# Operands of the seven-product MLP taken from one transposition of each row tile, and its start in a written order

## Chip, cores and metric

The kernel runs on one core of one Trainium2 chip. The metric is the device time of one execution in microseconds (us), the median of several runs of the same program. TensorE (PE) multiplies matrices and transposes 128x128 blocks, VectorE (DVE), ScalarE (ACT) and GpSimd (POOL) work on tiles, and the queue of SyncE (SP) issues the loads and stores.

## What is computed

The reference is an encoder of two layers on 1024 tokens of 1024 channels. Layer 0 begins with an attention over the tokens, layer 1 with a pooling mixer. Each layer then attends into 256 memory tokens (`memory_cross_attention`) and applies a gated MLP. The change lies in these last two steps:

```
def memory_cross_attention(h, mem_n, w_q, w_kv, w_o):
    q = (h @ w_q).reshape(b, s, X_HEADS, X_HEAD_DIM) * (X_HEAD_DIM ** -0.5)
    ...
    p = jax.nn.softmax(scores, axis=-1).astype(v.dtype)
    o = jnp.einsum('bhsm,bmhd->bshd', p, v).reshape(b, s, D_MODEL)
    return o @ w_o

def conv_gated_ffn(h, w_up, conv_w, conv_b, w_down):
    u = h @ w_up
    up = jnp.pad(u, ((0, 0), (1, 1), (0, 0)))
    u = up[:, :-2] * conv_w[0] + up[:, 1:-1] * conv_w[1] + up[:, 2:] * conv_w[2] + conv_b
    gate, val = u[..., :D_FF], u[..., D_FF:]
    return (jax.nn.silu(gate) * val) @ w_down

# per layer
    x = x + memory_cross_attention(rmsnorm(x, xattn_norm[i]), rmsnorm(mem, mem_norm[i]), ...)
    x = x + conv_gated_ffn(rmsnorm(x, ffn_norm[i]), ...)
```

All of it is float32. D_FF is 2816, so that `w_up` is 1024 x 5632: 22 blocks of 128 gate columns and 22 of value columns.

## The kernel before

**Arithmetic.** Each operand of a matrix product is kept as two float32 parts of fewer bits, `hi` and `lo`. `hi_lo` (L150) makes them: ACT copies the source to `hi` (L153), VectorE subtracts it from the source (L154). A product of 128x128 with 128x512 is then three matmuls in `mm3` (L230; hi·hi L233, hi·lo L234, lo·hi L235). The split operands lie in 20 slots of a pool `R`, raw data in six tiles `scr` and in the eight tiles `X` of the residual (128 tokens x 1024 channels each). PSUM has a pool `psA` of two tiles of two banks and `psB` of four banks.

**Cross-attention and output projection.** `cross` (L624 on) makes scores, softmax and values; what it returns is the transposed output, one group of slots for the first 512 tokens, one for the second. `project` (L248) multiplies it with `w_o`: for each column half n of `w_o` (loaded and split just before its use), for each of the 8 row tiles, 24 matmuls into one bank, and VectorE adds the bank to `X` (L261). In the second half each row tile is then stored to DRAM (`Xd`, L723), since the residual is needed again behind the MLP and its tile in SBUF is used up, and normed in place (square sum on ACT, GpSimd, VectorE L219). One tile later its blocks are transposed.

**The MLP by seven products.** `seven_into` (L706), `ffn` (L750) and `ffn_main` (L831) compute the up-projection with Strassen's scheme in Winograd's form. The weights of pair f (128 gate and 128 value columns) give A11, A12 (gate, first and second half of the channels), A21, A22 (value); the normed rows give B11, B21 (first 512 tokens, by channel half), B12, B22 (second 512 tokens). The sums are S1 = A21 + A22, S2 = S1 - A11, S4 = A12 - S2, S3 = A11 - A21, and T1 = B12 - B11, T2 = B22 - T1, T3 = B22 - B12, T4 = B21 - T2. Seven products of 12 matmuls each replace eight:

- p2 = A12·B21 goes to a bank of its own and is copied into the gate row (ACT)
- p1 = A11·B11 opens the bank z and is added to the gate row (VectorE, L817)
- p5 = S1·T1 opens the bank y and is copied into the value row (ACT, L879)
- p6 = S2·T2 accumulates in z; z is copied into the gate row (ACT, L882)
- p3 = S4·B22 accumulates in y; y is added to the gate row (VectorE, L885)
- p7 = S3·T3 accumulates in z; z is added to the value row (VectorE, L890)
- p4 = A22·T4 accumulates in z; z is copied into the value row (ACT, L896)

The two rows of 128 x 1024 then pass through the convolution (ACT L841, VectorE L842 and L843), SiLU (ACT L887) and the product of gate and value (VectorE L902), and are stored to DRAM as a row of `G` (L903). The order of the products of pair f is p1, p5, p6, p3, p7, p2 of pair f+1, p4. Between them stand the splits of the seven left operands of pair f+1 (`ahead`), and at the end of a pair the load of the weights of pair f+2 (L771, two tiles of 512 KB) and their four sums on GpSimd (L782 to L785).

**The operands on the right.** T1, T2, T3, T4 are made from the rows before they are transposed, on VectorE and GpSimd (`second`, L725 on). Seven operands of four tiles with four blocks each are transposed (L718), 112 blocks per layer; T3 and T4 come after the products p2 and p1 of pair 0 (`tail`). T2 has a tile of its own, `extra`.

**Behind it.** The down-projection (`down`, `operand` L849) takes G back from DRAM in rounds of four rows.

**What sets the order.** Most of the program is given to a scheduler, which sets the order of the instructions on each engine by its own costs; within an engine the queue is then fixed, and each instruction waits for what it reads and for buffers. Only parts under `manual_schedule` keep the order of the source.

## Time and profile before

| | |
|---|---|
| median of 3 runs | 2659.68 us (2658.92 to 2660.28) |
| the profiled execution | 2661.13 us, its span 2659.4 us |
| mean granted TensorE clock | 0.992 of full speed |
| TensorE matmuls and transposes | 2595.0 us, 98% of the span, 13913 instructions |
| TensorE weight loads | 2216.8 us, 83%, 13913 instructions |
| VectorE | 1720.5 us, 65%, 2291 instructions |
| ScalarE | 1207.8 us, 45%, 2024 instructions |
| GpSimd | 695.0 us, 26%, 709 instructions |
| DMA | 209.22 MB, mean 79 GB/s |

The span is the time between the first and the last event of the profiled execution; the time of the execution is a little longer. Busy shares are means over the whole span. The output projection and the start of the MLP lie near 845 to 1000 us in layer 0 and near 1870 to 2020 us in layer 1. A row of busy time by stretches has the bounds and the length of the stretch, then for PE, weight loads, VectorE, ScalarE and GpSimd the busy time with the number of instructions begun, then the granted clock (1.00 is full), the DMA share and the GB/s. A row of waits names the waiting instruction, behind the arrow what it waited for, and then the time in us, the number of waits and the longest. A row of instructions in a timeline has start, duration, engine, line, operation and tiles, the number of instructions that the row joins (their duration is then from the first start to the last end), and in brackets the idle time before it.

### The profile page before, as it was taken

Reading aid. Unit: us, or ns where it says so; the run is one execution under the profiler, and the core shown is the slowest. Engines: PE = TensorE matmul, PEld = TensorE weight load, DVE = VectorE, ACT = ScalarE, POOL = GpSimd, SP = SyncE. Lnnn points to the kernel's source line nnn. Section 1 sums busy time; section 2 is a strip of 40 time slices with the busy share of each in tenths; the row PEclk is TensorE's granted clock in tenths of the full one; section 3 lists DMA queues with packets and bytes.
Section 4 is the critical chain, followed back from the end, with each engine's and each line's share of the span. In section 5 each row is a group of like instructions: output and inputs, shape, how many; then the busy total and the mean of one; then the engine's idle time right before and its main releaser. Section 6 shows DMA issues by size and latency. Waiting matters only on the chain.

```text
span 2659.4 us, 36296 instructions
## 1 busy us (share of the span) xinstructions
PE 2595.0 (98%) x13913; PEld 2216.8 (83%) x13913; DVE 1720.5 (65%) x2291; ACT 1207.8 (45%) x2024; POOL 695.0 (26%) x709
## 2 busy tenths in 40 slices
PE   8989999999999999999999998999999999999998
PEld 7988888888898878888878888889878888887886
DVE  6779999955246387777765435425378777767434
ACT  4448888843135255454542205425245555444111
POOL 3664445521012153433300001102034333310001
PEclk9999999999999999999999999999999999999999
DMA  4200000032222132223254203322122232326201
GB/s 157 83 1 1 1 1 1 2 135 65 70 80 89 48 95 73 94 72 95 87 187 154 100 19 89 103 64 72 58 92 91 72 95 72 95 104 241 99 24 63
DMA packets 167554, 209.22 MB, mean 79 GB/s; under 512 B 6741, under 2 KB 134077, under 8 KB 167381
## 3 DMA queue, kind: packets, MB, share of 16 engines
q1 hardware_dynamic: 167381, 206.91, 23.4%
q8 instruction: 109, 1.79, 0.3%
q14 instruction: 64, 0.52, 0.1%
HBM read 166.42 MB, written 35.65 MB: 76 GB/s over the span
## 4 chain that ended last, share of the span: by engine, by line
PE 57%; DVE 2%; ACT 2%; DMA 1%; issue 1%; POOL 1%; SPq 0%; POOLq 0%; DVEq 0%; ACTq 0%
PE pB L234 18%; PE pB L233 18%; PE pB L235 18%; DVE R L154 1%; ACT R L153 1%; DMA scr<-X 0%; DMA scr<-G 0%; PE pA L998 0%; PE pA L233 0%; PE pA L234 0%; PE pA L235 0%; DVE scr L842 0%; PE pB L718 0%; POOL ms L206 0%; DVE scr L843 0%
## 5 line engine op out<-in xcount | busy, mean ns | idle before, releaser
L233 PE MATMUL pB<-R,R 128*128 128x512 f32 (+1 forms) x3088 | 1160.9, 377 | 16.5 <-ACT scr L879 9.6
L234 PE MATMUL pB<-R,R 128*128 128x512 f32 (+1 forms) x3088 | 1157.6, 375 | 4.3 <-DVE R L154 4.0
L235 PE MATMUL pB<-R,R 128*128 128x512 f32 (+1 forms) x3008 | 1125.6, 374 | 0.0
L233 PEld LDWEIGHTS pB<-R,R 128*128 128x128 f32 x3088 | 582.1, 189 | 127.6 <-ACT scr L879 10.4
L234 PEld LDWEIGHTS pB<-R,R 128*128 128x128 f32 x3088 | 582.7, 189 | 109.0 <-DVE R L154 7.5
L235 PEld LDWEIGHTS pB<-R,R 128*128 128x128 f32 x3008 | 567.5, 189 | 101.0 <-DVE R L154 0.4
L153 ACT ACTIVATE R<-scr 128x1024 fp32r<-128x1024 f32 (+1 forms) x186 | 185.7, 1024 | 353.0 <-PE pB L234 283.5
L154 DVE TENSOR_TENSOR R<-X,R 128x512 fp32r<-128x512 f32 x294 | 256.3, 885 | 63.6 <-ACT R L153 63.0
L153 ACT ACTIVATE R<-X 128x512 fp32r<-128x512 f32 x294 | 181.3, 630 | 245.4 <-PE pB L234 225.6
L922 DVE TENSOR_TENSOR X<-pB,X 128x512 f32<-128x512 f32 x192 | 130.9, 688 | 221.3 <-PE pB L235 221.2
L206 POOL TENSOR_SCALAR ms<-ss 128x1 f32<-128x1 f32 (+2 forms) x102 | 26.8, 263 | 909.0 <-ACT scr L214 422.4
L154 DVE TENSOR_TENSOR R<-scr,R 128x1024 fp32r<-128x1024 f32 (+1 forms) x186 | 218.0, 1194 | 49.5 <-ACT R L153 46.2
L153 ACT ACTIVATE R<-pB 128x512 fp32r<-128x512 f32 (+1 forms) x216 | 113.8, 556 | 185.3 <-PE pB L235 81.3
L227 PE MATMUL pB<-ident,scr 128*128 128x128 f32 x1376 | 182.4, 276 | 9.7 <-DVE scr L219 8.0
L227 PEld LDWEIGHTS pB<-ident,scr 128*128 128x128 f32 x1376 | 157.5, 142 | 36.5 <-POOL scr L319 14.6
L319 POOL TENSOR_SCALAR scr<-scr,inv 128x1024 f32<-128x1024 f32 x128 | 144.0, 1125 | 167.2 <-DVE inv L318 162.3
L154 DVE TENSOR_TENSOR R<-pB,R 128x512 fp32r<-128x512 f32 (+1 forms) x216 | 131.4, 636 | 76.9 <-ACT R L153 76.3
L842 DVE SCALAR_TENSOR_TENSOR scr<-scr,conv 128x1023 f32<-128x1023 f32 x88 | 139.4, 1584 | 62.4 <-ACT scr L841 62.0
L782 POOL TENSOR_TENSOR X<-X 128x512 f32<-128x512 f32 x42 | 56.2, 1339 | 447.0 <-DMA X<-in_ffn_w_up 447.0
L154 DVE TENSOR_TENSOR PT<-pB,PT 128x512 fp32r<-128x512 f32 x256 | 163.9, 680 | 3.3 <-ACT PT L153 2.4
L316 ACT ACTIVATE scr<-pA,nm 128x1024 f32<-128x1024 f32 x128 | 142.9, 1116 | 44.6 <-DVE nm L313 42.6
L313 DVE TENSOR_REDUCE nm<-pA 128x1 f32<-128x1024 f32 x128 | 156.1, 1220 | 0.9 <-PE pA L309 0.5
(123 smaller groups left out, 3188.7 us busy)
## 6 DMA issues: line engine op xcount, KB each, us to landing
X<-in_ffn_w_up SPq DMA_DIRECT2D x84, 512.0 KB
G<-scr SPq DMA_DIRECT2D x44, 512.0 KB
scr<-G SPq DMA_DIRECT2D x44, 512.0 KB
scr<-in_ffn_w_down SPq DMA_DIRECT2D x44, 512.0 KB
scr<-in_xattn_w_kv SPq DMA_DIRECT2D x32, 512.0 KB
scr<-in_attn_w_qkv SPq DMA_DIRECT2D x20, 512.0 KB
scr<-in_xattn_w_q SPq DMA_DIRECT2D x16, 512.0 KB
scr<-in_xattn_w_o SPq DMA_DIRECT2D x16, 512.0 KB
```

The source lines that it names most:

```text
L153: nc.scalar.activation(hi, src, AF.Copy)
L154: nc.vector.tensor_tensor(out=lo, in0=src, in1=hi.bitcast(F32), op=OP.subtract)
L227: self.nc.tensor.transpose(p[:, k, :], src[:, b * P:(b + 1) * P], self.ident)
L233: mm(out, ah, bh, start=start, stop=False)
L234: mm(out, ah, bl, start=False, stop=False)
L235: mm(out, al, bh, start=False, stop=stop)
L313: nc.vector.tensor_reduce(nm, s, axis=AX.X, op=OP.max, negate=True)
L316: nc.scalar.activation(pr, s, AF.Exp, bias=nm, accum_out=rs)
L319: nc.gpsimd.tensor_scalar(pr, pr, ri, 1.0, op0=OP.mult, op1=OP.mult)
L782: tt(out=b["S1"], in0=b["A21"], in1=b["A22"], op=OP.add)
L842: nc.vector.scalar_tensor_tensor(c[:, 1:], u[:, :S - 1], cv[:, 0, f:f + 1], c[:, 1:], op0=OP.mult, op1=OP.add)
L922: nc.vector.tensor_tensor(out=x, in0=p, in1=x, op=OP.add)
```

## The change

1. **Output projection tile by tile.** Both column halves of `w_o` are loaded and split ahead. The 16 steps (column half, row tile) go in the order written in `begin`. The add of the bank to `X` is as before; each complete tile is stored, normed and transposed one step later, once, both channel halves together: 64 blocks per layer.
2. **Operands from transposed blocks.** T1 to T4 are formed from the transposed blocks in PSUM and in the `X` tiles (`take1`, `take2`, `late`, `fourth`). The first 512 tokens of the scheme are now the even tiles, the second the odd ones. The rows of gate and value are in the order of the tokens, so the reads of the banks write 4 x 128 pieces (`half`, `put`, `add`). `extra` is dropped. The cross-attention's scores, transpositions and values follow the order even, odd.
3. **Start of the up-projection by hand.** `begin` writes out the order of splits, operand parts, products and reads of the banks (`read[...]`) through p4 of pair 0 and p5 of pair 1. Each product method returns the read of its bank as a function, which is called at another place. The sums of pair 1 are made on VectorE, those of all others on GpSimd as before.
4. **Up-projection in source order.** Pairs 0 to 20 stand under `manual_schedule`; only the last is left to the scheduler. p2 goes to `psA`, no longer to `psB`. The second convolution step, SiLU and the product of gate and value are placed behind other products (`conv1`, `conv2`, `gate`, `value`, `todo`); the load of pair f+2 comes at the first product of pair f, its sums S1, S2 behind p2 of pair f+1 and S4, S3 behind p4.

The diff, cut to its core (the removed functions stand above):

```
--- before
+++ after
...
+class Seven:
...
+    def rows(self, t):
+        self.nc.sync.dma_start(out=self.Xd[t * P:(t + 1) * P, :], in_=self.X[t])
+        self.r[t] = self.kn.row_rstd(self.X[t])
...
+    def norm(self, t):
+        x = self.X[t]
+        self.nc.vector.scalar_tensor_tensor(x, x, self.r.pop(t), self.gain, op0=OP.mult, op1=OP.mult)
...
+    def turn(self, t):
+        self.ps[t] = [self.kn.psB() for _ in range(2)]
+        for b in range(NK):
+            self.nc.tensor.transpose(self.ps[t][b // 4][:, b % 4 * P:(b % 4 + 1) * P],
+                                     self.X[t][:, b * P:(b + 1) * P], self.kn.ident)
...
+    def keep(self, name, t, src):
+        self.kn.hi_lo(*self.parts(name, t), src.rearrange("p (a b) -> p a b", a=4))
...
+    def late(self, name, t):
+        lo, hi = self.LO, self.HI
+        src = {"T2": self.X[t][:, hi], "T3": self.X[t][:, lo], "T4": self.X[t - 1][:, hi]}[name]
+        self.keep(name, t, src)
...
+    def take1(self, t):
+        nc, ps, lo, hi = self.nc, self.ps[t], self.LO, self.HI
+        x, y = self.X[t - t % 2], self.X[t]
+        nc.scalar.copy(y[:, lo], ps[0])
+        if t % 2:
+            self.sub(nc.vector, x[:, lo], ps[0], x[:, lo])
+            self.sub(nc.vector, y[:, hi], ps[1], x[:, lo])
+            self.sub(nc.vector, y[:, lo], ps[1], y[:, lo])
...
+    def take2(self, t):
+        nc, ps, lo, hi = self.nc, self.ps.pop(t), self.LO, self.HI
+        x, y = self.X[t - t % 2], self.X[t]
+        if t % 2 == 0:
+            nc.scalar.copy(y[:, hi], ps[1])
+            self.keep("B11", t, ps[0])
+            self.keep("B21", t, ps[1])
+        else:
+            self.keep("T1", t, x[:, lo])
+            self.keep("B22", t, ps[1])
+            if t < 4:
+                self.fourth(nc.gpsimd, t)
...
+    def fourth(self, e, t):
+        x, y, hi = self.X[t - 1], self.X[t], self.HI
+        self.sub(e, x[:, hi], x[:, hi], y[:, hi])
...
+    def sums(self, f, which=("S1", "S2", "S4", "S3"), e=None):
+        b = self.blocks(f)
+        how = {"S1": ("A21", "A22", OP.add), "S2": ("S1", "A11", OP.subtract), "S4": ("A12", "S2", OP.subtract),
+               "S3": ("A11", "A21", OP.subtract)}
+        for n in which:
+            p, q, op = how[n]
+            (e or self.nc.gpsimd).tensor_tensor(out=b[n], in0=b[p], in1=b[q], op=op)
...
+    def half(u, h):
+        return u.rearrange("p (t h c) -> p h t c", h=2, c=P)[:, h]
...
+    def put(self, u, h, p):
+        self.nc.scalar.copy(self.half(u, h), p.rearrange("p (t c) -> p t c", c=P))
...
+    def add(self, u, h, p):
+        u = self.half(u, h)
+        self.nc.vector.tensor_tensor(out=u, in0=p.rearrange("p (t c) -> p t c", c=P), in1=u, op=OP.add)
...
+    def p2(self, f):
+        x = self.kn.psA()[:, :512]
+        self.product(f, "A12", "B21", x, True)
+        u = self.bank[f] = {"g": self.kn.scr()}
+        return lambda: self.put(u["g"], 0, x)
...
+    def p6(self, f):
+        u = self.bank[f]
+        self.product(f, "S2", "T2", u["z"], False)
+        return lambda: self.put(u["g"], 1, u["z"])
...
+    def p3(self, f):
+        u = self.bank[f]
+        self.product(f, "S4", "B22", u["y"], False)
+        return lambda: self.add(u["g"], 1, u["y"])
...
+    def p7(self, f):
+        u = self.bank[f]
+        self.product(f, "S3", "T3", u["z"], False)
+        return lambda: self.add(u["v"], 1, u["z"])
...
+    def p4(self, f):
+        u = self.bank[f]
+        self.product(f, "A22", "T4", u["z"], False)
+        return lambda: self.put(u["v"], 0, u["z"])
...
+    def begin(self, gemm, add, free, between, gate, value):
+        late, split = self.late, self.split
+        steps = ((0, 0), (0, 2), (1, 0), (1, 2), (0, 4), (1, 4), (0, 6), (1, 6),
+                 (0, 1), (1, 1), (0, 3), (1, 3), (0, 5), (0, 7), (1, 5), (1, 7))
+        turns = {3: 0, 4: 2, 6: 4, 8: 6, 10: 1, 12: 3, 15: 5}
+        extras = {1: between, 2: lambda: self.load(0), 6: lambda: self.load(1, (0,)), 7: lambda: self.sums(0),
+                  14: lambda: (split(0, "A12", "A11"), late("T2", 1), late("T2", 3)),
+                  15: lambda: split(1, "A12", "A11")}
+        for i, (n, t) in enumerate(steps):
+            gemm(n, t)
+            free(n, t)
+            u = turns.get(i)
+            if u is not None:
+                self.turn(u)
+            extras.get(i, lambda: None)()
+            add(n, t)
+            if n:
+                self.rows(t)
+            if u is not None:
+                self.take1(u)
+            if n:
+                self.norm(t)
+            if u is not None:
+                self.take2(u)
+        dve = self.nc.vector
+        read = {2: self.p2(0), 1: self.p1(0)}
+        self.turn(t)
+        read[2]()
+        self.take1(t)
+        self.take2(t)
+        split(0, "S1")
+        read[2], read[0], read[5] = self.p2(1), self.p1(1), self.p5(0)
+        read[2]()
+        late("T2", t)
+        split(0, "S2")
+        read[1]()
+        late("T2", 5)
+        read[6] = self.p6(0)
+        split(0, "S4")
+        read[0]()
+        late("T3", 1)
+        late("T3", 3)
+        read[5]()
+        read[3] = self.p3(0)
+        late("T3", 5)
+        late("T3", 7)
+        read[6]()
+        split(0, "S3")
+        self.fourth(dve, 5)
+        self.fourth(dve, 7)
+        self.spare.extend(self.X[j] for j in (1, 3, 5))
+        self.load(1, (1,))
+        read[7] = self.p7(0)
+        late("T4", 1)
+        late("T4", 3)
+        read[3]()
+        late("T4", 5)
+        late("T4", 7)
+        self.spare.extend(self.X[j] for j in (7, 0, 2, 4, 6))
+        self.load(2)
+        split(0, "A22")
+        read[7]()
+        read[4] = self.p4(0)
+        self.sums(1, ("S1",), dve)
+        split(1, "S1")
+        gate[0]()
+        self.sums(1, ("S2",), dve)
+        split(1, "S2")
+        read[5] = self.p5(1)
+        read[4]()
+        self.sums(1, ("S4", "S3"), dve)
+        split(1, "S4")
+        gate[1]()
+        read[5]()
+        value[0]()
+        split(1, "S3", "A22")
+        value[1]()
+        self.sums(2)
+        del self.raws[0]
+        self.done(1)
...
-                for h in range(XH):
-                    R.put(qT[h, half])
+                R.put(*(qT[h, half] for h in range(XH)))
         def turn(t):
-            if t % 4 == 0:
-                PT[t // 4] = [R.get() for _ in range(4)]
-            self.transposed(prs.pop(t), self.put_T(PT[t // 4], t))
+            if t < 2:
+                PT[t] = [R.get() for _ in range(4)]
+            self.transposed(prs.pop(t), self.put_T(PT[t % 2], t // 2))
...
         for t in range(4):
-            scores(t)
+            scores(2 * t)
             memory_part(4 + t)
         for t in range(4):
-            scores(4 + t)
-            turn(t)
+            scores(2 * t + 1)
+            turn(2 * t)
         values(0, (0, 1))
-        turn(4)
+        turn(1)
         values(0, (2, 3))
+        turn(3)
         turn(5)
-        turn(6)
         values(0, (4, 5))
         turn(7)
...
-    def seven_into(self, X, gain, Xd):
...
+    def ffn(self, i, w, lhs, X, free, late):
+        nc, R, a = self.nc, self.R, self.a
+        Xd = self.tc.dram_tile([S, D], F32, name=f"Xd{i}")
+        U = Seven(self, a["ffn_w_up"][i], lambda f: (f * P, (NF + f) * P), X, Xd, self.bcast(a["ffn_norm"][i]))
+        def gemm(n, t):
+            ps[t] = self.psB()
+            for k in range(NK):
+                self.mm3(ps[t], *lhs(t, k), *self.blk(ws[n], k, slice(0, 512)), k == 0, k == NK - 1)
+        def add(n, t):
+            x = X[t][:, n * 512:(n + 1) * 512]
+            nc.vector.tensor_tensor(out=x, in0=ps.pop(t), in1=x, op=OP.add)
+        def freed(n, t):
+            if t == NT - 1:
+                R.put(*ws[n])
+            if n:
+                free(t)
+        ps = {}
+        ws = [self.load_rows(w, n) for n in range(2)]
+        return self.ffn_main(i, U, X, Xd, late, partial(U.begin, gemm, add, freed, self.conv_table(i)))
+    def ffn_main(self, i, U, X, Xd, late, begin):
+        nc, R = self.nc, self.R
+        wd = self.a["ffn_w_down"][i]
         G = self.tc.dram_tile([FF, S], F32, name=f"G{i}")
...
+        C = {}
+        def conv1(u, f):
+            c = C[f] = self.scr()
+            nc.scalar.activation(c, u, AF.Identity, scale=self.cv[:, 1, f:f + 1], bias=self.cv[:, 3, f:f + 1])
+            nc.vector.scalar_tensor_tensor(c[:, 1:], u[:, :S - 1], self.cv[:, 0, f:f + 1], c[:, 1:],
+                                           op0=OP.mult, op1=OP.add)
+        def conv2(u, f):
+            c = C[f]
+            nc.vector.scalar_tensor_tensor(c[:, :S - 1], u[:, 1:], self.cv[:, 2, f:f + 1], c[:, :S - 1],
+                                           op0=OP.mult, op1=OP.add)
+        def gate(f):
+            def finish():
+                conv2(U.bank[f]["g"], f)
+                nc.scalar.activation(C[f], C[f], AF.Silu)
+            return lambda: conv1(U.bank[f]["g"], f), finish
+        def value(f):
+            def finish():
+                c = C.pop(NF + f)
+                nc.vector.tensor_tensor(out=c, in0=c, in1=C.pop(f), op=OP.mult)
+                nc.sync.dma_start(out=G[f * P:(f + 1) * P, :], in_=c)
+            return (lambda: conv1(U.bank[f]["v"], NF + f), lambda: conv2(U.bank.pop(f)["v"], NF + f), finish)
...
+        def pair(f):
+            left = list(order)
+            nothing = lambda: None
             def ahead(n=1):
                 for _ in range(n):
                     if f + 1 < NF:
                         if left:
...
+                            U.split(f + 1, left.pop(0))
                             if not left:
...
+                                U.done(f + 1)
                     elif first:
                         operand(*first.pop(0))
...
+            g, v, before = gate(f), value(f), value(f - 1)
+            todo = ((U.p1, before[1] if f > 1 else nothing), (U.p5, before[2]), (U.p6, nothing), (U.p3, g[0]),
+                    (U.p7, g[1]), (lambda f: U.p2(f + 1) if f + 1 < NF else nothing, nothing), (U.p4, v[0]))
+            for j, (product, then) in enumerate(todo):
+                if f > 1 or j > 1:
+                    product(f)()
+                if f + 2 < NF:
+                    if j == 0:
+                        U.load(f + 2)
+                    elif j == 5:
+                        U.sums(f + 2, ("S1", "S2"))
+                    elif j == 6:
+                        U.sums(f + 2, ("S4", "S3"))
+                ahead((1, 1, 2, 0, 1, 1, 1)[j] if 1 < f < NF - 1 else (0, 0, 1, 0, 2, 2, 2)[j] if f == 1 else j != 5)
+                then()
+            if f == NF - 1:
+                v[1]()
+                v[2]()
+        with self.tc.manual_schedule():
+            begin(gate(0), value(0))
+            for f in range(1, NF - 1):
+                pair(f)
+        pair(NF - 1)
+        for s in U.H.values():
             R.put(*s)
...
+        free = list(U.spare)
...
```

More of the change, by code (lines that the diff above doesn't have):

```diff
@@ L857, in ffn_main @@
         order = ("A12", "A11", "S1", "S2", "S4", "S3", "A22")
-        load(1)
-        sums(1)
-        for f in range(NF):
-            u, left = bank[f], list(order)
+        def pair(f):
+            left = list(order)
+            nothing = lambda: None
             def ahead(n=1):
```

218 lines of the change are left out of this document (62 added, 156 removed).

## Prediction

> **What bounds the kernel now.** I read the page first, then busy time by stretches, then what TensorE waits for.
>
> ```profile
> PE 2595.0 (98%) x13913; PEld 2216.8 (83%) x13913; DVE 1720.5 (65%) x2291; ACT 1207.8 (45%) x2024; POOL 695.0 (26%) x709
> ```
>
> ```profile
> 900.00:1000.00 100.00, 93.44 (x453) 76.51 (x452) 77.71 (x88) 47.09 (x81) 44.54 (x38) 0.97 0.28 90
> ...
> 1100.00:1200.00 100.00, 100.00 (x442) 82.57 (x441) 74.67 (x79) 49.73 (x73) 35.67 (x21) 1.00 0.29 90
> ...
> 1900.00:2000.00 100.00, 93.64 (x460) 77.08 (x459) 60.12 (x74) 34.71 (x64) 30.99 (x32) 0.98 0.21 71
> ```
>
> The columns behind the stretch are its length, then busy time and count of PE, weight loads, VectorE (DVE), ScalarE (ACT), GpSimd (POOL), then the granted clock. TensorE is the bound. In the middle of an MLP it is busy for all of 100 us and starts 442 matmuls, 0.226 us each; so one of the seven products of a pair (12 matmuls) takes 2.72 us and one projection tile (24) takes 5.43 us. Only two things can shorten the kernel: fewer TensorE instructions, or fewer gaps. The change works where an output projection hands over to the MLP, and there, in both layers, 6.5 us of 100 are idle and the clock is not full. The waits of TensorE in the handover of layer 0 (first answer) and of layer 1 (second), in us, times, longest:
>
> ```profile
> PE pB L233 <- ACT scr L879: 4.8, 1, 4.8
> PE pB L233 <- DVE R L154: 1.6, 2, 0.8
> PE pB L718 <- DVE R L154: 0.6, 1, 0.6
> ```
>
> ```profile
> PE pB L233 <- ACT scr L879: 4.7, 1, 4.7
> PE pB L233 <- DVE R L154: 0.9, 1, 0.9
> PE pB L718 <- DVE R L154: 0.6, 1, 0.6
> PE pB L233 <- DVE scr L890: 0.3, 1, 0.3
> ```
>
> One of the two 0.8 us waits of layer 0 lies in the cross-attention, before the handover. So 4.8 + 0.8 + 0.6 = 6.2 us of gaps go with the old handover in layer 0, and 4.7 + 0.9 + 0.6 + 0.3 = 6.5 us in layer 1. The big one is the copy of a product's bank (line 879), which is queued on ACT behind splits that wait for GpSimd's sums of pair 1. It also costs clock (the column behind POOL's busy time):
>
> ```profile
> 963.00:964.00 1.00, 0.00 (x0) 0.00 (x0) 0.85 (x2) 0.82 (x2) 1.00 (x2) 0.98 0.00 0
> 964.00:965.00 1.00, 0.00 (x0) 0.00 (x0) 1.00 (x1) 1.00 (x3) 1.00 (x2) 0.50 0.55 163
> 965.00:966.00 1.00, 0.63 (x2) 0.54 (x3) 1.00 (x2) 1.00 (x3) 1.00 (x1) 0.50 1.09 330
> ...
> 970.00:971.00 1.00, 1.00 (x4) 0.76 (x4) 1.00 (x3) 0.49 (x1) 0.00 (x0) 0.61 0.47 137
> ```
>
> ```profile
> 1994.00:1995.00 1.00, 0.49 (x2) 0.41 (x3) 1.00 (x2) 1.00 (x3) 1.00 (x1) 0.89 1.08 324
> ...
> 1998.00:1999.00 1.00, 1.00 (x6) 0.81 (x5) 1.00 (x1) 0.03 (x1) 1.00 (x1) 0.90 0.02 6
> ```
>
> In layer 0 the clock is halved from the gap until 970.8, that is for 5.4 us after work resumes at 965.4: 2.7 us lost. In layer 1 it is halved from 1994.8 to 1998.2: 1.7 us lost.
>
> **What goes.** The old handover transposes seven operands of 4 tiles, 7 x 4 x 4 = 112 blocks; the new one transposes the 8 row tiles once, 64 blocks, and forms the sums after it. So 48 transposes go per layer. Price:
>
> ```profile
> 821.99 1.03 PE L227 MATMUL pB<-ident,scr 128*128 128x128 f32 x8
> 822.78 0.48 PE L233 MATMUL pB<-R,R 128*128 128x512 f32 x1
> 823.10 0.40 PE L234 MATMUL pB<-R,R 128*128 128x512 f32 x1
> ```
>
> Eight of them hold the queue from 821.99 to 822.78, and the first matmul behind them is 0.32 before its successor instead of 0.23: 0.88 us for eight, 0.11 each, 5.3 us per layer. TensorE bounds this stretch, so this comes off in full. With gaps and clock the old handover gives up 5.3 + 6.2 + 2.7 = 14.2 us in layer 0 and 5.3 + 6.5 + 1.7 = 13.5 in layer 1, **27.7 us** together, if nothing new is late.
>
> **What comes: new gaps, S per layer.** I laid the new order of each engine out by hand with these durations.
>
> ```profile
> 929.75 1.29 DVE L154 TENSOR_TENSOR R<-pB,R 128x512 fp32r<-128x512 f32 x2 [0.83 <-ACT R L153]
> ...
> 959.17 11.84 DVE L154 TENSOR_TENSOR R<-X,R 128x512 fp32r<-128x512 f32 x8
> ...
> 974.73 1.71 DVE L843 SCALAR_TENSOR_TENSOR scr<-scr,conv 128x1023 f32<-128x1023 f32 x1
> ...
> 981.67 1.28 DVE L842 SCALAR_TENSOR_TENSOR scr<-scr,conv 128x1023 f32<-128x1023 f32 x1
> ```
>
> ```profile
> 964.75 0.56 ACT L879 COPY scr<-pB 128x512 f32<-128x512 f32 x1
> ...
> 976.66 1.28 ACT L887 ACT_TABLE_LOAD   x1
> 977.95 1.06 ACT L887 ACTIVATE scr<-scr 128x1024 f32<-128x1024 f32 x1
> ...
> 980.39 1.24 ACT L841 ACTIVATE scr<-scr,conv 128x1024 f32<-128x1024 f32 x1
> ```
>
> ```profile
> 956.81 1.28 POOL L782 TENSOR_TENSOR X<-X 128x512 f32<-128x512 f32 x1 [6.80 <-DMA X<-in_ffn_w_up]
> ...
> 968.26 1.60 POOL L784 TENSOR_TENSOR X<-X,X 128x512 f32<-128x512 f32 x1
> ```
>
> A 128x512 operation on VectorE follows the last after 0.6 us; if it reads two operands in SBUF while GpSimd computes (956.8 to 969.9) it takes 1.48 (eight in 11.84). A conv step takes 1.28 alone and 1.71 beside GpSimd. The 4x128 pieces of the new interleaved views are those that the splits of before already write, so they get the same price.
> [...]
>
> *Projection.* Steps are still 5.43 us and a tile is transposed one step after its second half, as before, so the same chain must fit: sum, store, norm.
>
> ```profile
> 907.60 0.69 DVE L261 TENSOR_TENSOR X<-pB,X 128x512 f32<-128x512 f32 x1 [1.88 <-PE pB L235]
> ...
> 911.05 1.29 DVE L219 SCALAR_TENSOR_TENSOR X<-X,rs,scr 128x1024 f32<-128x1024 f32 x1 [0.17 <-DMA Xd<-X]
> ```
>
> The norm waits for the store to DRAM and is done 4.74 us after the gemm; odd tiles add 5 VectorE operations (3 us), which run after it. That fits, with a few tenths now and then: 0.3. The extra wait is at the last tile. Count from the end of the last projection matmul (0). VectorE still does norm 5 and two splits, so the sum of tile 7 ends at 1.3; its squares (1.2 us on ACT) stand ahead of the copy of tile 5's bank, so tile 5's three differences end at 5.2 and norm 7 at 6.4, while TensorE (transposes of tile 5, products p2 and p1 of pair 0) is free at 6.4 or a little earlier: 0.5.
> *p4 of pair 0.* TensorE does tile 7, p2 and p1 of pair 1, p5, p6, p3, p7 of pair 0 and is done at 23.7. p4 accumulates into the bank that p7's sum reads, with no product between. That sum is queued on VectorE behind nine operations starting at 19.45 (the split of S3 can't start before p6's copy), at 0.6 each: it runs from 24.85 to 25.55. Gap 1.9. (Without the queue, 0.8: the sum itself.)
> *p6 and p3 of pair 1.* From 25.5 VectorE makes S1, splits it, does a conv step, S2, its split, S4, S3, S4's split, the second conv step; three of these wait for ACT's half of a split. Without GpSimd S2 is ready at 31.2, when p6 starts; with it (loads issued at about 22 land 4 us later, see below) 2.2 later: I take 1.1. The copy of p5's bank, which p3 needs, stands behind SiLU in ACT's queue: conv step done at 34.3 to 37.0, then table load 1.28, SiLU 1.06, copy 0.57: p3 starts 3.4 to 3.8 late: 3.6. Behind that copy stand on ACT value conv and splits, which p7 and p4 of pair 1 wait for through VectorE.
> *After it.* The value conv and the product hold VectorE, so p2 of pair 2 and p4 of pair 1 wait 1.0 (0.65 to 2.8), and p6 of pair 2 waits for p1's sum, 1.7 (to 3.1).
>
> ```profile
> 1099.94 0.37 SPq L771 DMA_DIRECT2D X<-in_ffn_w_up  x1
> ```
>
> ```profile
> 1103.89 1.30 POOL L782 TENSOR_TENSOR X<-X 128x512 f32<-128x512 f32 x1 [13.20 <-DMA X<-in_ffn_w_up]
> ```
>
> These two give the 4 us of a load. SP's queue holds the same stores and loads, in a new order; the first part of pair 1 is loaded far ahead, its second part is issued at 16 and is there at 20, before 25.5, so it costs nothing.
> S = 0.3 + 0.5 + 1.9 + 1.1 + 3.6 + 1.0 + 1.7 = **10.1 us**, bounds 3 (only the sum ahead of p4 and short waits) and 14.6 (GpSimd beside all of it: 0.8 + 1.9 + 2.2 + 3.8 + 2.8 + 3.1).
>
> *Pairs 2 to 20.* No instruction is added. p4 needs p7's sum, and p2 of the next pair (2.72 us) lies between, as before:
>
> ```profile
> PEld pB L233 <- DVE scr L890: 1.0, 3, 0.4
> ```
>
> In 300 us of before only weight loads waited, 1.0 us in all. The new order has no split between p3's sum and the conv step, but SP loads behind A22's split, so GpSimd's sums fall on splits and the product ahead of it. By my layout p7's sum ends 0.5 before p4 at a mean slowdown and 0.4 after it if each operation is slowed as in the row of eight. Taken as 0; bound 0.4 x 19 x 2 = 15 us.
> *Cross-attention.* Even and odd tiles instead of halves: same instructions, slots come free two score tiles later; 0, give or take 1 us.
>
> **Sum.** The profiled execution took 2661.1 us, 1.4 over the median shown. 2661.1 - 27.7 + 2 x 10.1 = 2653.6; on the median that is **2652 us** (-0.3%).
>
> **Rivals.**
> B, VectorE keeps up: the lists drain faster than I laid them out and only some 3 us per layer stay. 2659.7 - 27.7 + 6 = 2638. For it: VectorE is at 60 to 78% there. Against: the wait behind the table load is in ACT's order.
> C, the gap only moves: GpSimd's sums of pair 2 collide with VectorE's of pair 1; S = 14.6, 2659.7 - 27.7 + 29.2 = 2661. For it: the 1.48 us row. Against: GpSimd starts late in the list. If the 3.8 us gap also halves the clock, as 4.8 and 4.7 did, up to 2 x 2.7 more, 2667.
> [...]
> D, slower: in pairs 2 to 20 p4 waits for p7's sum, 0.4 us each, because GpSimd now runs beside the splits ahead of it. 2652 + 15 = 2667. It decides against the change from 0.2 us a pair on (7.7 us). For it: slack of half a microsecond. Against: before holds the same wait with no gap.
> That the change does not do what it says can only mean that the gaps stay, which is C: the blocks and the orders are in the instruction lists.
>
> **Chances.** A (2652) 0.40, B 0.20, C 0.20, D 0.20. A measurement tells about 0.2% (5.3 us). Faster: B and nine tenths of A, 0.56; same: the rest of A and most of C, 0.20; slower: D and C with the clock, 0.24. Range 2634 to 2668: B with a little less, up to D. A's own range is 2644 to 2657.
>
> **What would show it.** Transposes in the handover: 64 per layer and no row for `extra`. TensorE waiting for ACT's bank copy at p3 of pair 1, behind the table load, 3 to 4 us once per layer; for VectorE's sum at p4 of pair 0, near 2 us; clock 1.00 there. Pairs 2 to 20: 442 matmuls per 100 us. Wrong if those stretches fall under 438, if a gap over 4 us with the clock at 0.5 remains, or if the projection steps themselves wait.

## The result and the profile after

The changed kernel takes 2728.78 us in the median (2726.98 to 2730.3), the kernel before beside it 2659.98: the ratio is 1.0258, interval 1.0240 to 1.0275. It is **slower by 69 us** where 8 us less were forecast, and outside the range. The span of its profiled execution is 2727.1 us. The page of the changed kernel, first part:

```profile
PE 2600.1 (95%) x13817; PEld 2206.8 (81%) x13817; DVE 1797.3 (66%) x2311; ACT 1206.8 (44%) x2048; POOL 662.9 (24%) x689
```

The 96 transposes are gone (13913 instructions became 13817), but TensorE's share fell from 98 to 95%, and VectorE has 77 us more work although it has only 20 instructions more. Busy time by stretches of the changed kernel:

```profile
1200.00:1300.00 100.00, 92.11 (x401) 74.58 (x400) 78.72 (x73) 44.58 (x68) 29.95 (x19) 1.00 0.25 75
...
1300.00:1380.00 80.00, 73.70 (x321) 59.70 (x320) 62.97 (x58) 35.81 (x54) 25.85 (x15) 1.00 0.28 86
1380.00:1400.00 20.00, 20.00 (x90) 16.57 (x89) 14.13 (x18) 8.83 (x13) 0.00 (x0) 1.00 0.47 165
```

Most of the loss is not at the handover. In the middle of the MLP, where 442 matmuls per 100 us were started before, there are 401. And this loss ends by itself: as soon as GpSimd has no more sums to make (POOL 0.00, from 1380 us on), TensorE is full again. Counted by the timeline, p4 of pairs 2 and 19 start at 1014.34 and 1338.69 us before and at 1016.64 and 1372.49 after. That is 19.08 and **20.93 us a pair**; these 17 pairs lose 31.5 us in layer 0 and 31.7 in layer 1. From the first matmul of the projection to p4 of pair 2 it takes 168.1 us before and 170.2 after in layer 0, 167.8 and 169.4 in layer 1. So each handover gives about 2 us of loss, and the steady pairs nearly all the rest.

What TensorE waits for from 1100 to 1300 us (in all, times, longest), which was empty before:

```profile
PE pB L485 <- DVE scr L238: 15.8, 10, 1.6
```

Line 238 is the sum that VectorE makes from a bank; here it is p7's, and p4 waits for it once in every pair. In the same stretch VectorE waits for nothing but ScalarE (25.0 and 16.2 us), and no engine waits for GpSimd. VectorE's groups of instructions from 1100 to 1300 us show where its time went, in the kernel before (first) and in the changed one (second):

```profile
L154 DVE TENSOR_TENSOR R<-X,R 128x512 fp32r<-128x512 f32 x73 | 60.0, 833 | 16.7 <-ACT R L153 16.7
L842 DVE SCALAR_TENSOR_TENSOR scr<-scr,conv 128x1023 f32<-128x1023 f32 x21 | 34.0, 1618 | 13.5 <-ACT scr L841 13.4
...
L902 DVE TENSOR_TENSOR scr<-scr 128x1024 f32<-128x1024 f32 x11 | 13.4, 1217 | 0.0
```

```profile
L406 DVE TENSOR_TENSOR R<-X,R 128x512 fp32r<-128x512 f32 x68 | 76.6, 1137 | 25.0 <-ACT R L405 25.0
...
L1007 DVE SCALAR_TENSOR_TENSOR scr<-scr,conv 128x1023 f32<-128x1023 f32 x19 | 24.4, 1284 | 16.2 <-ACT scr L1006 16.2
L1024 DVE TENSOR_TENSOR scr<-scr 128x1024 f32<-128x1024 f32 x9 | 20.8, 2315 | 0.0
```

The split's lo part rose from 833 to 1137 ns and the product of gate and value from 1217 to 2315, while the convolution step fell from 1618 to 1284. GpSimd makes the same four sums, but beside other instructions. The order of one pair in the changed kernel, VectorE's timeline (first) and GpSimd's (second):

```profile
1212.29 0.68 DVE L238 TENSOR_TENSOR scr<-pB,scr 128x512 f32<-128x512 f32 x1
...
1214.68 1.78 DVE L406 TENSOR_TENSOR R<-X,R 128x512 fp32r<-128x512 f32 x1
1216.38 2.31 DVE L1024 TENSOR_TENSOR scr<-scr 128x1024 f32<-128x1024 f32 x1
1218.62 3.47 DVE L406 TENSOR_TENSOR R<-X,R 128x512 fp32r<-128x512 f32 x2
1222.02 0.68 DVE L238 TENSOR_TENSOR scr<-pB,scr 128x512 f32<-128x512 f32 x1
1224.01 1.28 DVE L1007 SCALAR_TENSOR_TENSOR scr<-scr,conv 128x1023 f32<-128x1023 f32 x1 [1.31 <-ACT scr L1006]
1225.21 0.69 DVE L238 TENSOR_TENSOR scr<-pB,scr 128x512 f32<-128x512 f32 x1
```

```profile
1214.40 1.51 POOL L208 TENSOR_TENSOR X<-X 128x512 f32<-128x512 f32 x1 [13.79 <-DMA X<-in_ffn_w_up]
1215.99 5.56 POOL L208 TENSOR_TENSOR X<-X,X 128x512 f32<-128x512 f32 x3
```

GpSimd is busy from 1214.4 to 1221.6. In just that time VectorE makes three splits and the product, 7.3 us instead of 3.0. Behind them stands p3's sum (1222.02), 3.1 us after p3 ended (its last matmul starts at 1218.54); behind that the convolution step, which waits for ScalarE; and behind that p7's sum (1225.21), for which p4 waits. In the kernel before, VectorE and GpSimd at the same place:

```profile
1199.75 0.69 DVE L885 TENSOR_TENSOR scr<-pB,scr 128x512 f32<-128x512 f32 x1 [1.66 <-PE pB L235]
```

```profile
1199.32 1.31 POOL L782 TENSOR_TENSOR X<-X 128x512 f32<-128x512 f32 x1 [13.07 <-DMA X<-in_ffn_w_up]
```

There GpSimd starts when p3's sum is due, and VectorE had been waiting 1.66 us for TensorE. What it slows stands behind p3's sum (the convolution step at 1201.76 takes 1.65 us).

Three theories follow. Theory 1: GpSimd's place beside VectorE's list is the cost. Theory 2: the order alone, p7's sum behind a step that waits for ScalarE. Theory 3: VectorE simply has too much work.

### The profile page after: what moved, and what is told of

Read it like the earlier page. It is cut to its first block, busy times and chain, and to the rows that moved or that the text cites. A ratio compares the mean times of both kernels' runs of the same rounds, so it can differ in the third digit from the quotient of the medians.

```text
span 2727.1 us, 35986 instructions
## 1 busy us (share of the span) xinstructions
PE 2600.1 (95%) x13817; PEld 2206.8 (81%) x13817; DVE 1797.3 (66%) x2311; ACT 1206.8 (44%) x2048; POOL 662.9 (24%) x689
## 4 chain that ended last, share of the span: by engine, by line
PE 50%; DVE 27%; ACT 11%; issue 7%; POOL 2%; DMA 2%; SPq 0%; DVEq 0%; ACTq 0%; POOLq 0%
PE pB L486 13%; PE pB L485 13%; PE pB L487 13%; DVE R L406 10%; ACT scr L1006 4%; DVE scr L1012 4%; DVE scr L1024 3%; PE pB L479 3%; DVE scr L238 3%; DVE nm L565 2%; PE pA L561 2%; ACT R L405 2%; ACT scr L1018 1%; ACT scr L234 1%; PE pB L792 1%
## 5 line engine op out<-in xcount | busy, mean ns | idle before, releaser
L485 PE MATMUL pB<-R,R 128*128 128x512 f32 (+1 forms) x2912 | 1098.1, 379 | 81.7 <-DVE scr L238 65.5
L486 PE MATMUL pB<-R,R 128*128 128x512 f32 (+1 forms) x2912 | 1091.9, 375 | 2.4 <-DVE R L406 2.0
L487 PE MATMUL pB<-R,R 128*128 128x512 f32 (+1 forms) x2832 | 1059.6, 374 | 0.0
L485 PEld LDWEIGHTS pB<-R,R 128*128 128x128 f32 x2912 | 550.4, 189 | 200.6 <-DVE scr L238 70.6
L486 PEld LDWEIGHTS pB<-R,R 128*128 128x128 f32 x2912 | 551.5, 189 | 100.9 <-DVE R L406 5.9
L487 PEld LDWEIGHTS pB<-R,R 128*128 128x128 f32 x2832 | 535.8, 189 | 95.2 <-DVE R L406 0.4
L406 DVE TENSOR_TENSOR R<-X,R 128x512 fp32r<-128x512 f32 x322 | 340.8, 1073 | 106.3 <-ACT R L405 106.1
L208 POOL TENSOR_TENSOR X<-X,X 128x512 f32<-128x512 f32 x120 | 219.2, 1840 | 6.3
L405 ACT ACTIVATE R<-X 128x512 fp32r<-128x512 f32 x322 | 196.9, 629 | 25.7 <-DVE X L208 19.0
L1006 ACT ACTIVATE scr<-scr,conv 128x1024 f32<-128x1024 f32 x88 | 109.3, 1242 | 187.6 <-DVE scr L238 187.5
L1007 DVE SCALAR_TENSOR_TENSOR scr<-scr,conv 128x1023 f32<-128x1023 f32 x88 | 114.1, 1296 | 79.3 <-ACT scr L1006 79.3
```

The costliest lines, as they stand in the source:

```text
L208: (e or self.nc.gpsimd).tensor_tensor(out=b[n], in0=b[p], in1=b[q], op=op)
L405: nc.scalar.activation(hi, src, AF.Copy)
L406: nc.vector.tensor_tensor(out=lo, in0=src, in1=hi.bitcast(F32), op=OP.subtract)
L485: mm(out, ah, bh, start=start, stop=False)
L486: mm(out, ah, bl, start=False, stop=False)
L487: mm(out, al, bh, start=False, stop=stop)
```

## The experiments

**Order alone.** p7's sum ahead of the convolution step:

```
         def conv1(u, f, step=True):
             ...
             nc.scalar.activation(c, u, AF.Identity, ...)
-            nc.vector.scalar_tensor_tensor(c[:, 1:], ...)
+            if step: conv1b(u, f)
 ...
             def finish():
+                if not step: conv1b(U.bank[f]["g"], f)
                 conv2(U.bank[f]["g"], f)
```

> The changed kernel with one order changed in the steady pairs: p7's sum stands ahead of VectorE's first convolution step of the gate row, not behind it. The time before it is 2728.8 us; a pair takes 20.93 us instead of 19.05, with 1.58 us of wait at p4 for p7's sum, 18 times a layer. Theory 1 (GpSimd's sums slow the splits and the gate-value product that stand ahead of p3's sum, and the list from p3's sum over convolution, SiLU and p1's sum back to p3's sum is a closed circle that is longer than TensorE's seven products): the wait at p4 goes, but the circle is only shortened by p7's sum and the split behind it, 1.2 to 1.3 us, so a pair takes 19.6 to 19.8 us, a wait for p1's sum appears at p6 instead, and the time is about 2728.8 - 36 x 1.25 = 2684 us (2675 to 2695). Theory 2 (only the order is at fault, p7's sum behind a step that waits for ScalarE): the wait goes and nothing takes its place, 19.05 us a pair, about 2661 us. Theory 3 (VectorE has too much work in a pair, whatever the order): no change, 2729.

Measured: 2728.77 us, ratio 1.0254 (1.0239 to 1.0269), the time that theory 3 gave; but the wait at p4 went, as theories 1 and 2 said. VectorE's timeline, and behind it TensorE's wait, which is now at p6 for p1's sum:

```profile
1218.80 1.27 DVE L238 TENSOR_TENSOR scr<-pB,scr 128x512 f32<-128x512 f32 x2
1221.31 0.69 DVE L406 TENSOR_TENSOR R<-X,R 128x512 fp32r<-128x512 f32 x1 [1.23 <-ACT R L405]
1221.92 1.28 DVE L1012 SCALAR_TENSOR_TENSOR scr<-scr,conv 128x1023 f32<-128x1023 f32 x1
1223.23 1.28 DVE L1017 SCALAR_TENSOR_TENSOR scr<-scr,conv 128x1023 f32<-128x1023 f32 x1
```

```profile
1209.90 0.47 PE L485 MATMUL pB<-R,R 128*128 128x512 f32 x1 [1.42 <-DVE scr L238]
```

The two sums now run together (1218.80), but the split behind them waits 1.23 us for ScalarE, whose hi part stands behind its convolution step. From p3's sum to the end of the second step it takes 5.7 us as before (1218.80 to 1224.5, in the changed kernel 1222.02 to 1227.7). This is a **closed circle** without TensorE: p3's sum, convolution, SiLU, value convolution, p1's sum, second step, splits and product, p3's sum of the next pair. It takes 20.93 us in every pair of the changed kernel, and TensorE waits wherever it meets it. In this run most pairs still take 20.9 to 21.0 us and some 19.0 to 19.9; why some turns are shorter was not followed up. Theory 2 falls, and so does theory 1's number: of the 1.25 us to be saved in a pair only 0.3 came in layer 0 and 0.5 in layer 1 (means of 20.63 and 20.39 us), so most of it was not on the circle. That the time is the same to the microsecond is luck: the steady pairs won 14 us, and 12 us were lost behind pair 19, where TensorE waits longer for splits; the mean granted clock of the run was 0.988, in the changed kernel 0.990.

**GpSimd's place alone.** The load of pair f+2 behind p3 instead of p1; no instruction of VectorE, ScalarE or TensorE moves.

```
-                    if j == 0:
+                    if j == 3:
                         U.load(f + 2)
```

> The changed kernel with the load of pair f+2 issued behind p3 of pair f instead of p1, that is behind the store of G in SyncE's queue, so that GpSimd's sums fall later, behind the splits and the gate-value product. The order of VectorE, ScalarE and TensorE is untouched. Theory 1 (GpSimd beside the splits and the product ahead of p3's sum): those take 0.6 and 1.2 us again, p3's sum comes 3 us earlier, the sums fall on convolution steps and two other splits instead; a pair takes 19.05 to 19.4 us, 2661 to 2673 us. Theory 2 (only VectorE's order): the wait at p4 stays, 2725 to 2730. Theory 3 (VectorE has too much work): GpSimd slows as many operations as before, so 2720 to 2730.

Measured: 2673.93 us, ratio 1.0048 (1.0032 to 1.0065): 55 of the 69 us are gone. GpSimd (first) now begins 11.2 us behind p1's sum (1198.5) instead of 2.1 us, and VectorE (second) is quick in front of p3's sum:

```profile
1209.65 2.21 POOL L208 TENSOR_TENSOR X<-X 128x512 f32<-128x512 f32 x1 [12.18 <-DVE R L406]
```

```profile
1220.64 1.21 DVE L1024 TENSOR_TENSOR scr<-scr 128x1024 f32<-128x1024 f32 x1
1222.62 1.29 DVE L406 TENSOR_TENSOR R<-X,R 128x512 fp32r<-128x512 f32 x2 [0.78 <-ACT R L405]
1224.19 0.69 DVE L238 TENSOR_TENSOR scr<-pB,scr 128x512 f32<-128x512 f32 x1 [0.28 <-PE pB L487]
```

A pair takes 19.2 us in layer 0 (17 pairs in 326.7) and 19.4 in layer 1. p3's sum waits for TensorE again, as before. This is theory 1, 0.9 us above its range. Theory 3 falls, since VectorE has the same instructions.

**No GpSimd in the steady pairs.** The sums of pairs 3 to 21 on VectorE:

```
-                        U.sums(f + 2, ("S1", "S2"))
+                        U.sums(f + 2, ("S1", "S2"), nc.vector)
 ...
-                        U.sums(f + 2, ("S4", "S3"))
+                        U.sums(f + 2, ("S4", "S3"), nc.vector)
```

> The changed kernel with the four sums of pairs 3 to 21 made on VectorE, not on GpSimd, at the places where they stand in the source (behind p2 of the next pair and behind p4). VectorE gets four operations of 0.6 us more in a pair; nothing is slowed by GpSimd any more. Theory 1 (GpSimd slows VectorE): the three splits and the product get 3 x 1.1 + 1.1 = 4.4 us shorter, 2.4 us are added, partly where VectorE waits for ScalarE; a pair takes 19.05 us and the time is 2661 us (2658 to 2668). Theory 2 (only the order): the wait at p4 stays, 2725 or more. Theory 3 (VectorE has too much work): longer by up to 36 x 2.4 us, 2730 to 2815.

Measured: 2656.59 us, ratio 0.9980 (0.9971 to 0.9989). VectorE got four instructions more per pair and the kernel 72 us faster. That is 1.4 us below theory 1's range, which did not count what the handover gives. A stretch, and VectorE's group of splits from 1100 to 1300 us:

```profile
1200.00:1300.00 100.00, 100.00 (x443) 82.81 (x442) 79.27 (x101) 48.25 (x73) 0.00 (x0) 1.00 0.27 79
```

```profile
L406 DVE TENSOR_TENSOR R<-X,R 128x512 fp32r<-128x512 f32 x73 | 49.2, 687 | 24.7 <-ACT R L405 24.7
```

VectorE is as busy as in the changed kernel (79%), with 101 instructions instead of 73 in 100 us. This kernel is also the handover by itself: 165.7 and 165.4 us from the first projection matmul to p4 of pair 2, 2.4 less than before.

**GpSimd at work for nobody.** The same kernel with four additions per pair on GpSimd into a tile `extra` that nothing reads:

> The kernel with the sums on VectorE, and beside them four additions of the same size on GpSimd in each of the pairs 3 to 21, at the same place as GpSimd's sums in the changed kernel, into a tile that nothing reads. Nobody waits for their result. Theory 1 (GpSimd slows VectorE's operations beside it): two splits, a third and the product take 1.1 us more each again, of which VectorE's idle time of about 1.5 us a pair absorbs a part; a pair takes 21 to 22 us instead of 19.05, 2728 to 2765. Rival (what cost time in the changed kernel was waiting for GpSimd's sums or for their place in the order): 2657.

Measured: 2670.25 us, ratio 1.0035 (1.0022 to 1.0049), 13.7 us more than without them. Work whose result nobody waits for costs time, so the rival falls (in the changed kernel, too, no engine waits for GpSimd from 1100 to 1300 us); but it is at most a fifth of what theory 1 gave. Some 10 of the 13.7 us come ahead of p4 of pair 2: from the first projection matmul it takes 170.6 us in both layers, against 165.7 and 165.4 without the additions. A steady pair takes 19.2 us instead of 19.04. GpSimd (first) and VectorE (second):

```profile
1218.79 2.54 POOL L1069 TENSOR_TENSOR extra<-X,X 128x512 f32<-128x512 f32 x1 [12.11 <-DMA X<-in_ffn_w_up]
```

```profile
1218.95 1.22 DVE L1024 TENSOR_TENSOR scr<-scr 128x1024 f32<-128x1024 f32 x1
1220.94 2.38 DVE L406 TENSOR_TENSOR R<-X,R 128x512 fp32r<-128x512 f32 x2 [0.78 <-ACT R L405]
```

Here the product keeps its 1.22 us and GpSimd's addition beside it takes 2.54. In this pair only two splits and, at 1206.07, one convolution step (1.70) are slowed. The place is not quite that of the changed kernel: GpSimd begins 2.8 us behind p1's sum, not 2.1, and the split ahead of the product is done before it (0.68 us). In the changed kernel the product beside GpSimd took 2.31 us; here it is GpSimd's addition that takes longer (the first sum of a pair took 1.31 us in the kernel before and 1.51 in the changed one), and the expectation had put the cost on VectorE each time. GpSimd's addition starts 0.16 us ahead of the product by the profile, whose spans on GpSimd are rough. What decides which of the two takes longer is not shown.

**The handover: one place or the whole list?** In the changed kernel TensorE's waits there were:

```profile
966.16 0.47 PE L485 MATMUL pB<-R,R 128*128 128x512 f32 x1 [2.00 <-DVE scr L238]
980.86 0.50 PE L485 MATMUL pB<-R,R 128*128 128x512 f32 x1 [4.62 <-ACT scr L234]
...
991.50 0.50 PE L485 MATMUL pB<-R,R 128*128 128x512 f32 x1 [0.56 <-DVE scr L238]
...
1003.84 0.47 PE L485 MATMUL pB<-R,R 128*128 128x512 f32 x1 [3.88 <-DVE scr L238]
```

These are p4 of pair 0, p3 and p4 of pair 1, p6 of pair 2. The second waits for p5's bank copy behind SiLU (1.06 us) and its table load (1.28 us). On the kernel with the sums on VectorE the copy was put first:

```
-        gate[1]()
         read[5]()
+        gate[1]()
```

> The kernel with the sums on VectorE, and beside it in the start of the MLP the copy of p5's bank (pair 1) ahead of the second convolution step and SiLU, once per layer. In the changed kernel p3 of pair 1 waits 4.62 us for this copy, behind the table load and SiLU, and the clock is halved afterwards. To be compared with the kernel with the sums on VectorE alone. Theory A (the copy's place is the cost): the wait at p3 falls to about 0.6 us, no half clock there, 5 to 6 us per layer, 10 to 12 us less in all. Theory B (the list of VectorE and ScalarE around SiLU sets the pace, the gap only moves): p7 of pair 1 waits for the split of S3, p4 for p7's sum, and p6 of pair 2 waits longer; the time falls by 0 to 4 us.

Measured: 2655.54 us against 2656.59, not to be told apart. Theory B. TensorE's two waits:

```profile
975.99 0.50 PE L485 MATMUL pB<-R,R 128*128 128x512 f32 x1 [0.23 <-ACT scr L234]
982.50 0.80 PE L485 MATMUL pB<-R,R 128*128 128x512 f32 x1 [3.50 <-ACT scr L234]
```

4.6 us at p3 became 0.2 there and 3.5 one product later. The next run exchanged two pairs of steps ahead of p4 of pair 0 (`split(0, "S3")` with `read[6]()`, `read[7]()` with `split(0, "A22")`):

> The kernel with the sums on VectorE and, of the reordering, the two exchanges ahead of p4 of pair 0 alone: the split of S3 ahead of the copy of p6's bank (VectorE waited 1.4 us for ScalarE there), p7's sum ahead of the split of A22. The wait at p4 falls from 2.0 to about 0.7 us in both layers and the clock is not halved behind it. Theory B (VectorE and ScalarE set the pace of what follows, and their list is 1.4 us earlier): 1.4 us per layer less, the later waits longer by the clock that is won, 2653 to 2655. Theory A (each wait stands by itself): 1.3 us of wait and 1.5 us of clock per layer less, 2651.

Measured: 2654.44 us, ratio 0.9975 (0.9966 to 0.9984), theory B's value: p4 waits 0.88 us instead of 2.00, p6 of pair 1 1.87 instead of 0.80. The last step named in part 3 of the change, the sums of pair 1 on VectorE, was undone alone (`sums(1, ...)` on GpSimd):

> The kernel with the sums on VectorE (2656.6 us), with the four sums of pair 1 back on GpSimd at the same places, so that the first pairs' sums are as in the kernel before. VectorE has four operations of 0.6 us less there. If GpSimd slows VectorE (theory 1), its sums start when the second weight tile lands, some 4 us ahead of p4 of pair 0, and lengthen the splits of T4 and p7's sum's predecessors by about 1.1 us each: the wait at p4 grows from 2.0 to 4 to 6 us, and the times falls back by 2 to 4 us per layer less the 2.4 us given up: 2656 to 2665. Rival (VectorE's list is what counts, so four operations less help): 2.4 us per layer less, 2652.

Measured: 2656.33 us, ratio 0.9983 (0.9974 to 0.9993), no difference from 2656.59. TensorE's waits in it:

```profile
969.48 0.76 PE L485 MATMUL pB<-R,R 128*128 128x512 f32 x1 [5.74 <-DVE scr L238]
980.86 0.50 PE L485 MATMUL pB<-R,R 128*128 128x512 f32 x1 [0.57 <-ACT scr L234]
```

The wait at p4 grows to 5.7 us, as theory 1 said, and the 4.6 us at p3 are gone: the list is as long either way. What shortens it is to take work out of it. The next kernel has the two exchanges, puts pair 0's first convolution steps behind the splits of pair 1, the second steps and SiLU behind p6 and the product behind p3 of pair 1, and makes pair 2's sums on VectorE (lines joined; the two exchanges and the places in `pair` are left out):

```
-        self.sums(1, ("S1",), dve); split(1, "S1"); gate[0](); self.sums(1, ("S2",), dve); split(1, "S2")
-        read[5] = self.p5(1); read[4](); self.sums(1, ("S4", "S3"), dve); split(1, "S4")
-        gate[1](); read[5](); value[0](); split(1, "S3", "A22"); value[1](); self.sums(2)
+        self.sums(1, ("S1", "S2"), dve); split(1, "S1", "S2")
+        read[5] = self.p5(1); self.sums(1, ("S4", "S3"), dve); read[4](); split(1, "S4", "S3")
+        read[5](); split(1, "A22"); gate[0](); value[0]()
 ...
```

> The kernel with the sums on VectorE (2656.6 us), with the start of the MLP reordered in both layers: the split of S3 ahead of the copy of p6's bank, p7's sum ahead of the split of A22 (pair 0); behind p4 of pair 0 the sums and splits of pair 1 come first, and pair 0's convolution, SiLU and product only behind p6 and p3 of pair 1; the sums of pair 2 on VectorE too. In the kernel that it is made from, TensorE waits there 2.0, 0.8 + 0.3, 4.6 and 1.7 us, and the clock is halved for some 3.5 us behind the waits of 2.0 and 4.6. Theory B (pair 0's convolution and SiLU with the table load, and GpSimd's sums of pair 2 beside them, are what holds the chain of VectorE and ScalarE back): the wait at p4 falls to 0.7 us and the others to some tenths, no halved clock, 9 to 13 us per layer less: 2633 us (2630 to 2640). Rival (the work put off only comes back in pairs 1 and 2): waits of the same sum there, 2648 to 2657.

Measured: **2643.73 us**, ratio 0.9937 (0.9924 to 0.9949). Better than both kernels, between theory B and its rival: the handover takes 159.0 us instead of 165.7, 6.7 less per layer instead of 9 to 13. A part of the backlog came back:

```profile
964.73 0.47 PE L480 MATMUL pB<-R,R 128*128 128x512 f32 x1 [0.88 <-DVE scr L238]
983.28 0.57 PE L480 MATMUL pB<-R,R 128*128 128x512 f32 x1 [1.86 <-DVE scr L238]
994.65 0.47 PE L480 MATMUL pB<-R,R 128*128 128x512 f32 x1 [1.30 <-DVE scr L238]
```

The last run moved the backlog behind the sums that TensorE waits for (in pairs 1 and 2 product and convolution behind p7's sum, value convolution of pair 1 and sums of pair 3 behind p1's sum):

> The kernel with pair 0's convolution put off (2643.7 us), in which TensorE still waits 1.9 us at p4 of pair 1 for p7's sum and 1.3 and 2.9 us at p6 of pair 2 for p1's sum, because VectorE has product, convolution, sums and splits in front of these sums. Here the two sums come first and that work behind them: in pairs 1 and 2 the product of the pair before and the convolution step stand behind p7's sum, the value convolution of pair 1 and the sums of pair 3 behind p1's sum of pair 2. Theory B (VectorE has 16.8 us of work for 19.05 us of a pair, so a backlog costs nothing if nothing stands in front of the sums that TensorE waits for): these waits go and no halved clock is left there, 1.9 + 1.3 and 1.9 + 2.9 us and one half clock of 1.6 us, 2634 to 2637 us. Rival (the backlog is what TensorE waits for, wherever it stands): the same waits in pairs 2 and 3, 2641 to 2645.

Measured: 2640.61 us, ratio 0.9925 (0.9911 to 0.9938). The wait at p4 of pair 1 went; 1.6 us at p6 of pair 2 stayed and 1.3 us at p6 of pair 3 came. So the rival is nearer: its waits are there, and the time is 0.4 us below its range. 3 us were won of the 7 to 10 expected, because p1's sum now stands behind a split whose hi part is queued on ScalarE behind SiLU, as VectorE's timeline shows:

```profile
991.21 0.69 DVE L401 TENSOR_TENSOR R<-X,R 128x512 fp32r<-128x512 f32 x1 [2.19 <-ACT R L400]
991.82 0.68 DVE L238 TENSOR_TENSOR scr<-pB,scr 128x512 f32<-128x512 f32 x1
```

## Why the prediction was wrong, step by step

- **What goes** (48 transposes per layer) is right by the instruction count. The cross-attention at 0 is right: the projection's first matmul starts at 846.23 us before and at 846.46 after.
- **S, the new gaps**, was put at 10.1 us per layer. The waits in layer 0 sum to 2.00 + 4.62 + 0.56 + 3.88 = 11.1 us, at the places named; the smaller ones named (0.3, 0.5, 1.1) hardly showed. p3's wait was 4.6 instead of 3.6, and p6's of pair 2 3.9 instead of 1.7, with GpSimd's sums of pair 3 (until 995.4 us) beside VectorE's work ahead of it, where a convolution step at 994.14 took 2.31 us; it was 1.7 in the kernel with the sums on VectorE.
- **The clock** was forecast at 1.00 there, and that failed. It was halved behind three of the four waits in layer 0, once behind a wait of only 2.0 us:

```profile
968.00:969.00 1.00, 1.00 (x4) 0.76 (x3) 0.56 (x1) 0.41 (x1) 1.00 (x1) 0.50 0.52 125
982.00:983.00 1.00, 1.00 (x4) 0.81 (x3) 1.00 (x1) 1.00 (x3) 0.00 (x0) 0.50 0.00 0
1006.00:1007.00 1.00, 1.00 (x4) 0.80 (x3) 1.00 (x1) 0.00 (x0) 0.92 (x2) 0.50 0.00 0
```

  Some 3.4 us each at half speed (967.61 to 971.02, 981.26 to 984.67 and 1005.15 to 1008.57 us) are 1.7 us lost, 5 us together. 11.1 + 5 against the 14.2 us given up makes about 2 us of loss, and 2.1 is measured. In layer 1 the same sum makes 3 (10.0 us of waits, 6.5 of clock, 13.5 given up) where 1.6 is measured, so it is good to a microsecond or two. Rival C had this term once.
- **Pairs 2 to 20**, "taken as 0; bound 0.4 x 19 x 2 = 15 us", is **the step that failed**. The mechanism is rival D, which had a chance of 0.20; its price of 0.4 us a pair measured 1.85. Two reasons. First, the slowed operations were priced too low: the sum took a mean slowdown, and the bound the row of eight (1.48), while all four met GpSimd and a split took 1.73 and the product 2.31. For three splits that is 0.75 us a pair more than in the bound. Second, the layout followed one pair that began on time. p3's sum is itself late, and with it the convolution, the splits and the place where the next pair begins; the pairs after it don't start from zero. The circle of 20.9 us sets the pace, and no slack of 0.5 us at one wait says anything on it.
- "Before holds the same wait with no gap", the argument against D, was true and no argument: before, the sums fell behind p3's sum, not ahead of it.
- The signs named for being wrong (under 438 matmuls per 100 us) were the right ones.

## What to carry to other kernels

When a hand-written order replaces a scheduler's, look at where an engine that is off the critical path starts, not only at how long its work is: here a load issued a few microseconds earlier put GpSimd beside the wrong four instructions, and its place alone was worth 55 us. For a steady loop, follow the list of the helping engines once around, from an instruction to itself in the next turn, and compare that circle with the bound engine's time per turn; slack at a single wait does not tell it. And when moving one instruction only moves the wait, the list is the limit: take work out of it, or put it behind what the bound engine waits for (the last run won 3 us by this, not the 7 to 10 expected).

## What the runs showed of the hardware that was not expected

- In the changed kernel, in the pair shown, a product of 128x1024 beside GpSimd took 1.1 us more on VectorE, as much as a split of 128x512 (2.31 against 1.22, 1.73 against 0.6). With GpSimd at work for nobody the product kept its 1.22 us. A sum that reads a bank kept its 0.68 us, though GpSimd was busy beside it: in the run with pair 1's sums on GpSimd, VectorE (first) and GpSimd (second) have

```profile
965.78 0.68 DVE L238 TENSOR_TENSOR scr<-pB,scr 128x512 f32<-128x512 f32 x1
966.38 1.75 DVE L406 TENSOR_TENSOR R<-X,R 128x512 fp32r<-128x512 f32 x2
```

```profile
963.71 3.27 POOL L208 TENSOR_TENSOR X<-scr,X 128x512 f32<-128x512 f32 x2
```

- The length of a wait does not settle whether the clock is halved. In the kernel with pair 0's convolution put off, it was halved behind the wait of 1.86 us at 983.28 and not behind one of 2.90 us in layer 1:

```profile
2015.99 0.47 PE L480 MATMUL pB<-R,R 128*128 128x512 f32 x1 [2.90 <-DVE scr L238]
```

```profile
980.15:983.56 3.41, 1.55 (x7) 1.01 (x6) 3.41 (x5) 1.63 (x3) 0.00 (x0) 1.00 0.37 153
983.56:986.97 3.41, 3.41 (x9) 2.66 (x9) 3.41 (x6) 0.05 (x1) 0.00 (x0) 0.50 0.17 44
2010.98:2014.39 3.41, 2.10 (x10) 1.41 (x8) 3.41 (x7) 3.41 (x7) 0.00 (x0) 1.00 0.00 0
2014.39:2017.80 3.41, 1.81 (x8) 1.55 (x9) 3.41 (x5) 0.62 (x2) 0.00 (x0) 1.00 0.52 154
```

  In the trace of the changed kernel the clock changes at 967.61, 971.02, 981.26, 984.67, 1005.15 and 1008.57 us. These times are 3.41, 10.24, 3.41, 20.48 and 3.41 us apart, that is 1, 3, 1, 6 and 1 times 3.41, and each row above has that length. The wait of 1.86 us lies in one row and leaves TensorE 1.55 us of work in it; in the next row the clock is 0.50. The wait of 2.90 us is shared by two rows with 2.10 and 1.81 us of work, and the clock stays at 1.00. In the changed kernel TensorE had 1.44, 0.40 and 1.31 us of work in the 3.41 us ahead of the three halvings (from 964.19, 977.85 and 1001.74 us on); it had 1.81 and 1.63 us in those from 974.43 and 998.33 us on, and the clock stayed at 1.00 behind them. That is what was measured at these waits; what sets the clock in general is not shown.
